# Gate sigmoids and attention tasks given a place in the issue order of an encoder block

## The chip, the cores and the metric

One Trainium2 chip, one of its cores. The metric is the device time of one execution in microseconds (us); times of a kernel are medians of several runs. The profile is of one execution, taken by the hardware profiler. A core has a matrix engine (TensorE, PE in the profile, with its weight loads as PEld), a vector engine (VectorE, DVE), a scalar engine for activation functions (ScalarE, ACT), a general one (GpSimd, POOL) and SyncE (SP), which issues transfers here. Each engine takes its instructions in the order of its own queue; between engines semaphores hold an instruction until its inputs are there.

## The reference

One layer of an encoder block on 256 tokens of width 2048, all in float32:

```
h = rmsnorm(x);  proj = h @ w_in          # q,k,v (sb) | q,k,v (ca) | gate_sb | gate_ca
y_sb = stick_breaking_attention(q, k, v)  # 8 heads of 128, strictly causal
y_ca = chunked_relpos_attention(q, k, v)  # 8 heads of 128, softmax with a relative bias
merged = sigmoid(gate_sb) * (y_sb @ w_sb_out) + sigmoid(gate_ca) * (y_ca @ w_ca_out)
x = x + merged @ w_mix_out
x = x + (silu(g) * u) @ w_ffn_out,  g, u = split(rmsnorm(x) @ w_ffn_in)
x = x + sigmoid(rmsnorm(x) @ w_ple_gate) * (p @ w_ple_in)
out = rmsnorm(x)
```

The stick-breaking weights are `exp(log_sigmoid(z) + sum of log_sigmoid(-z) over the keys between)`, so they need a logarithm and exponentials; the chunked attention needs the exponential of a softmax; the gates need sigmoids.

## The kernel before

**Pieces.** Every matmul with a weight matrix is cut into pieces of a weight: 256 x 512 or 512 x 256 numbers, 512 KB, loaded by SP into one of the `raw` buffers. To keep float32 precision a piece is split in two: ACT rounds it (`hi`, lines 270, 285, 288 and 291, the "weight casts"), DVE subtracts (`lo`, line 250 in `minus`), and PE does three products, high by high, low by high and high by low, in `three` (lines 299 to 301). `hi` and `lo` have three buffers each (line 245), a fourth in some stages.

**Kinds of groups.** `group("row", ...)` makes 512 output columns for all tokens with `three`. `group("feat", ...)` makes queries and keys with the features on the partitions; it issues its own two matmuls per tile (lines 373 and 375) and does not call `three`. `unit(...)` makes two blocks of 512 columns with one multiplication in eight saved for some pairs of pieces (Strassen's scheme, `split_pair` and `pair_products`); `su` are the accumulators of its own products, and it has more DVE work per matmul. A `gate_unit` is a unit that makes gate or value columns.

**Order in the code.** `flush(every)` goes through the pieces that are queued: `prefetch` loads and splits up to two pieces ahead, `products` issues the matmuls, and after every `every` pieces one entry of the list `tasks` is run, that is, its instructions are written there. With `in_turn=True` the entry's instructions are written inside `tc.issue_after(state["mm"].ins)`. That context adds an order edge: whatever the block writes for the same engine as the given instruction is queued behind it there. It is no wait for its result, and instructions of the block for other engines get no edge. `state["mm"]` is set in `three` (line 301) and, for the very first piece, in line 363. `state["cast"]` is set in `split` (line 270), to the last weight cast written.

**Order on the chip.** The framework plans each engine's queue before the program runs: it goes through the instructions with a model of their times, and an engine takes the earliest-written instruction that is ready in the model. An instruction that is ready long before its place in the code may so be queued far ahead of it. A load of an activation table (ACT_TABLE_LOAD in the profile) is put in front of an ACT instruction whose function is not in the set that is loaded at that point; the loads are shown under the line of that instruction. Line 83 loads the set `natural_log_exp_and_others` at the start.

**The stages around the change**, in the order of the code:
- the first gate group (lines 863 and 864), then queries and keys of the first stick-breaking half, `queries_and_keys(0, 0, sb_tasks)`, with `flush(4)`. When its last piece is done its attention is appended to `tasks` as six entries, `s1, s2, s3` for heads 0 and 1 and again for heads 2 and 3; the first of them is still run by this flush;
- a first `gate_unit` (values and gate columns), `flush(None)`: no tasks;
- `queries_and_keys(0, 1, ...)` and `(1, 0, ...)`, in whose flushes the other attention entries of the halves before are run (`flush(3)`, `flush(2.67)`, and `drain(6)` for what is left but the newest six);
- four more gate units, no tasks;
- `queries_and_keys(1, 1, ...)`, with the tasks of the first chunked half;
- the output projections `w_sb_out` (m = 0), with the tasks of the last chunked half, and `w_ca_out` (m = 1). After each group of 512 columns, `out_post(m, c)` writes two sigmoids (line 909), two products of the projection with the gate (line 911, DVE) and, for m = 1, the sum (line 914) and the transposes for the next stage.

The steps of the stick-breaking attention: `s1` makes the scores `zp` (PE), the absolute value, `Exp` and `Ln` (ACT, lines 708 to 710), then on DVE lines 712 and 713, and the split of the result; `s2` the sums over later keys (`bt`, lines 721 to 726), line 727 on DVE and an `Exp` (line 728); `s3` the weighted values `yp`. The chunked attention has one `Exp` step in `s1` (line 767, four instructions) and two transfers of the bias on POOL's queue.

Of the kernel before, what the change touches and what calls it, by code (L numbers as in the profile page):

```python
# [11 lines left out]
AF = mybir.ActivationFunctionType  # L12
# [33 lines left out]
def block_kernel(ctx: ExitStack, tc: tile.TileContext, x, p, w_in, w_sb_out, w_ca_out, w_mix_out,  # L46
# [18 lines left out]
    nc = tc.nc  # L65
# [81 lines left out]
    def run_task():  # L147
        name, fn = tasks.popleft()
        fn()
        if name is not None:  # L150
            done.add(name)

    def group(kind, wsrc, n0, kts, lhs, post, needs=lambda kt: None, row0=0, keep=None, after=None):

        ncol, nk = (NB, 2) if kind == "row" else (FB, 4)
        g = dict(kind=kind, post=post, lhs=lhs, ps=None, keep=keep, after=after)
        kts = list(kts)
        for j in range(0, len(kts), nk):
            part = kts[j : j + nk]
            r = (row0 + j) * P  # L160
            pieces.append(dict(
                g=g, kts=part, ncol=ncol, first=j == 0, last=j + nk >= len(kts),
                src=[wsrc[r : r + len(part) * P, n0 : n0 + ncol].rearrange("(k p) n -> p k n", p=P)],
                needs=[k for k in (needs(kt) for kt in part) if k is not None],
            ))
# [164 lines left out]
    def products(pc):  # L330
        g = pc["g"]
        if pc.get("pair"):
            pair_products(pc)
        elif g["kind"] == "unit":
            if pc["first"]:
                state["hold"] = g["hold"]
                g["ps"] = g.get("ps", []) + banks(g, g["pool"], "mm", 2)
            for i, kt in enumerate(pc["kts"]):
                a, z = pc["first"] and i == 0, pc["last"] and i == 1
                for t in range(2):  # L340
                    row_products(g["ps"][2 * pc["block"] + t], g["lhs"], kt, t, pc["hi"][:, i, :], pc["lo"][:, i, :], a, z)
            if g["after"] is not None and pc["block"] == 1:
                g["after"](pc["kts"])
            if pc["last"]:
                g["post"](g, pc["block"])
                state["hold"] = g["hold"] and pc["block"] == 0
        elif pc is pieces[1]:
            with tc.issue_after(state["mm"].ins):
                group_products(pc)
        else:  # L350
            group_products(pc)
        del pc["hi"], pc["lo"]
# [29 lines left out]
    state = dict(loaded=0, split=0, at=0, raw=0, hl=0, ext=0, ps=ps_mm, fourth=None, ring=0, places=0, hold=False)  # L382
# [6 lines left out]
    def prefetch():  # L389
        while state["loaded"] < len(pieces) and state["raw"] + len(pieces[state["loaded"]]["src"]) <= RAW + state["places"]:  # L390
            load(pieces[state["loaded"]])
            state["loaded"] += 1
        room = 2 if state["at"] < 4 + KD // 2 else 4 if state["fourth"] is not None else 3
        while state["split"] < state["loaded"] and state["split"] <= state["at"] + 3:
            pc = pieces[state["split"]]
            if state["split"] > state["at"] and sum(map(size, pieces[state["at"] : state["split"] + 1])) > room:
                break
            behind = [started["p"]]
            if pc["g"] is pieces[4]["g"]:
                behind += started.get(pc["kts"][0] - 2, [])  # L400
            with ExitStack() as order:
                for i in behind:
                    order.enter_context(tc.issue_after(i.ins))
                split(pc)
            state["split"] += 1

    def drain(left=0):
        while len(tasks) > left:
            run_task()

    def later(fn, n=3):

        for _ in range(n):
            tasks.append((None, lambda: None))
        tasks.append((None, fn))

    def flush(every=1, until=None, in_turn=False):

        n = 0
        while state["at"] < len(pieces) and (until is None or until not in done):  # L420
            pc = pieces[state["at"]]
            prefetch()
            products(pc)
            state["at"] += 1
            n += 1
            if tasks and every and not state["hold"] and int(n / every) > int((n - 1) / every):
                if in_turn:
                    with tc.issue_after(state["mm"].ins):
                        run_task()
                else:  # L430
                    run_task()
# [21 lines left out]
    def into_table(dst, c, src, gain=None, key=None, forms=None, pool=None, pairs=PAIRS):  # L453


        n = ps_ax[-1][1] // S if pool is None else 2
        for k0 in range(0, 4, n):
            ps = (aux("tp") if pool is None else late["ps"][pool].tile([P, 512], F32, tag="mm", name="tp"))
            ps = ps.rearrange("p (k s) -> p k s", k=n)
            for k in range(n):  # L460
                for t in range(NT):
                    nc.tensor.transpose(ps[:, k, t * P : (t + 1) * P], src[:, t, (k0 + k) * P : (k0 + k + 1) * P], ident)  # L462
            step = n if forms is None else 2
            for k1 in range(0, n, step):
                table_part(dst, 4 * c + k0 + k1, ps[:, k1 : k1 + step, :], gain, forms, pairs)
        for k in range(4):
            done.add((key, 4 * c + k))
# [335 lines left out]
    def queries_and_keys(mixer, b, make):  # L803
        c0 = mixer * 3 * W + b * NB
        qT, kT = (mp.tile([P, 4, S], F32, tag=f"{n}{b}", name=n) for n in ("qT", "kT"))
        for dst, off, sc in ((qT, 0, SCALE), (kT, W, None)):
            for j in range(2):
                then = None
                if off and j == 1:
                    then = lambda t=make(qT, kT, (mixer, b), 4 * b): push_attention(*t)  # L810
                group("feat", w2, c0 + off + j * FB, range(KD), T1, feat_post(dst, 2 * j, sc, then), needs=hneed)
# [67 lines left out]
    flush(None)  # L879
    state["fourth"] = None  # L880
    queries_and_keys(0, 1, sb_tasks)
    flush(3)
    drain(6)
    queries_and_keys(1, 0, ca_tasks)
    flush(2.67)
    drain(6)

    four_buffers(1)
# [7 lines left out]
    for c in range(4):  # L896
        dma_x.dma_start(x_[:, :, c * NB : (c + 1) * NB], xr[:, :, c * NB : (c + 1) * NB])
    queries_and_keys(1, 1, ca_tasks)
    flush(2.67)
    drain(6)  # L900
    work = mp.tile([P, 1024], F32, tag="v0", name="work")

    def out_post(m, c):
        def post(ps):
            cs = slice(c * NB, (c + 1) * NB)
            gt = gates[:, :, m, cs]
            for t in range(NT):
                by = rstd if (m, c) == (1, 0) else r1
                nc.scalar.activation(gt[:, t, :], gt[:, t, :], AF.Sigmoid, scale=by["mix"][:, t : t + 1])
            for t in range(NT):  # L910
                nc.vector.tensor_tensor(gates[:, t, m, cs], ps[t], gates[:, t, m, cs], ALU.mult)
            if m == 1:
                mg = gates[:, :, 0, cs]
                nc.vector.tensor_tensor(mg, mg, gt, ALU.add)
                later(lambda: into_table(T1, c, mg, key="mg", forms=lambda kt: FP[:, kt // 4 - 2], pairs=MIX_PAIRS))
        return post

    for m, wo in ((0, w_sb_out), (1, w_ca_out)):
        for c in range(4):
            group("row", wo[0], c * NB, range(8 * m, 8 * m + 8), T2, out_post(m, c), needs=lambda kt: ("y", kt))  # L920
        state["places"] = 0
        flush(2.67 if m == 0 else 1)


    def residual_done(c, key):
# [263 lines left out]
```

## Time and profile before

| | us |
|---|---|
| median of 3 runs | 1463.69 (1462.29 to 1463.74) |
| the profiled execution | 1464.04 |
| its span, first to last instruction | 1462.3 |
| PE busy | 1447.8 (99%) |
| DVE busy | 1242.2 (85%) |
| ACT busy | 819.6 (56%) |

The span is what the trace covers; some 1.7 us of the execution lie around it. Busy times of engines overlap. A row `line engine op out<-in` names the line of the code and the tiles that are written and read; `<-` behind a time in brackets names what ended the idle time. For PE the end of a matmul is modelled, and matmuls overlap, so the start times say more than the durations.

### The profile page before, as it was taken

To read this page: it belongs to the slowest core of one execution; us is meant where nothing else is said; L and a number is where in the kernel's file an instruction comes from. 1 tells how busy PE (TensorE), PEld (TensorE's weight loads), DVE (VectorE), ACT (ScalarE), POOL (GpSimd) and SP (SyncE) were. 2 spreads that over 40 slices of the span, in tenths; PEclk is the share of its full clock that TensorE was granted. 3 is DMA by queue.
4 is the path that set the end of the run, shared out by engine and by line. 5 is a ranking of instruction groups with operands and counts; after the bars stand their busy time and mean duration, and the time that the engine had idled before them with its cause. 6 is when DMAs were issued, how large, how long until landed. Compare 5 with 4: busy or idle time off the path is not lost.

```text
span 1462.3 us, 18695 instructions
## 1 busy us (share of the span) xinstructions
PE 1447.8 (99%) x6849; PEld 1210.3 (83%) x6849; DVE 1242.2 (85%) x1570; ACT 819.6 (56%) x966; POOL 22.5 (2%) x44
## 2 busy tenths in 40 slices
PE   9999999999999999999999999999999999999997
PEld 7887888788888888888888888888888888888886
DVE  6978777998877777888999999999999989999775
ACT  6546567656555544565555555555645555565552
POOL 0100000000000000000000000000000000000000
PEclk9999999999999999999999999999999999999999
DMA  9865555566675555765666666666666666666672
GB/s 319 274 204 177 185 168 171 171 211 204 199 254 164 179 166 181 229 198 177 195 194 188 195 208 214 196 195 209 195 199 202 203 190 198 216 197 210 229 228 72
DMA packets 164731, 291.17 MB, mean 199 GB/s; under 512 B 9024, under 2 KB 42096, under 8 KB 164384
## 3 DMA queue, kind: packets, MB, share of 16 engines
q1 hardware_dynamic: 162528, 281.32, 61.5%
q0 software_dynamic: 2112, 8.68, 1.8%
q8 instruction: 53, 0.87, 0.3%
q14 instruction: 38, 0.31, 0.1%
HBM read 284.19 MB, written 5.77 MB: 198 GB/s over the span
## 4 chain that ended last, share of the span: by engine, by line
PE 96%; DMA 2%; ACT 1%; DVE 1%; issue 0%; SPq 0%; DVEq 0%; ACTq 0%
PE mm L300 23%; PE mm L301 23%; PE mm L299 23%; PE mm L373 8%; PE su L300 4%; PE su L301 4%; PE su L299 4%; PE mm L375 4%; PE tp L462 1%; DMA raw<-in_w_in 1%; DMA raw<-in_w_ple_in 1%; ACT hi L270 0%; DMA raw<-in_w_mix_out 0%; DVE lo L250 0%; PE yp L689 0%
## 5 line engine op out<-in xcount | busy, mean ns | idle before, releaser
L250 DVE TENSOR_TENSOR lo<-raw,hi 128x1024 fp32r<-128x1024 f32 (+1 forms) x517 | 625.7, 1218 | 131.1 <-ACT hi L270 120.8
L270 ACT CAST hi<-raw 128x1024 fp32r<-128x1024 f32 (+1 forms) x387 | 405.1, 1050 | 399.3 <-PE mm L301 299.0
L300 PE MATMUL mm<-lo,T 128*128 128x512 f32 x1349 | 526.2, 390 | 1.2 <-DVE lo L250 1.2
L301 PE MATMUL mm<-hi,T 128*128 128x512 f32 x1349 | 522.2, 390 | 0.0
L299 PE MATMUL mm<-hi,T 128*128 128x512 f32 x1349 | 500.4, 391 | 1.4 <-ACT hi L270 1.3
L299 PEld LDWEIGHTS mm<-hi,T 128*128 128x128 f32 x1349 | 252.9, 188 | 54.1 <-ACT hi L270 2.3
L300 PEld LDWEIGHTS mm<-lo,T 128*128 128x128 f32 x1349 | 253.3, 188 | 53.4 <-DVE lo L250 1.6
L301 PEld LDWEIGHTS mm<-hi,T 128*128 128x128 f32 x1349 | 253.3, 188 | 52.4
L373 PE MATMUL mm<-T,hi 128*128 128x512 f32 x512 | 180.4, 398 | 0.0
L375 PE MATMUL mm<-T,lo 128*128 128x256 f32 x512 | 140.3, 280 | 0.0
L373 PEld LDWEIGHTS mm<-T,hi 128*128 128x128 f32 x512 | 95.1, 188 | 20.7
L288 ACT CAST hi<-raw 128x1024 fp32r<-128x1024 f32 x65 | 68.5, 1053 | 77.2 <-DVE raw L250 25.4
L250 DVE TENSOR_TENSOR T<-xf,T 128x1536 fp32r<-128x1536 f32 x58 | 101.7, 1754 | 10.4 <-ACT T L291 10.4
L250 DVE TENSOR_TENSOR xf<-raw 128x512 f32<-128x512 f32 x130 | 89.1, 685 | 14.9 <-DMA raw<-in_w_ffn_in 4.2
L375 PEld LDWEIGHTS mm<-T,lo 128*128 128x128 f32 x512 | 96.6, 189 | 1.7
L291 ACT CAST T<-xf 128x1536 fp32r<-128x1536 f32 x58 | 85.9, 1480 | 18.8 <-DVE xf L250 18.1
L285 ACT CAST hi<-raw 128x1024 fp32r<-128x1024 f32 x65 | 68.5, 1053 | 31.5 <-PE mm L301 24.9
L834 DVE TENSOR_TENSOR C<-su,C 128x512 f32<-128x512 f32 x72 | 47.6, 682 | 0.3
L838 DVE TENSOR_TENSOR C<-mm,C 128x512 f32<-128x512 f32 x72 | 46.6, 680 | 0.0
L250 DVE TENSOR_TENSOR xf<-raw,xf 128x512 f32<-128x512 f32 x65 | 44.5, 685 | 0.4
L250 DVE TENSOR_TENSOR raw<-raw 128x512 f32<-128x512 f32 x65 | 44.5, 684 | 0.2
L301 PE MATMUL mm<-T,T 128*128 128x512 f32 (+1 forms) x90 | 33.4, 371 | 0.0
(326 smaller groups left out, 1448.0 us busy)
## 6 DMA issues: line engine op xcount, KB each, us to landing
raw<-in_w_ffn_in SPq DMA_DIRECT2D x176, 512.0 KB, 4.0
raw<-in_w_in SPq DMA_DIRECT2D x160, 512.0 KB, 4.3
raw<-in_w_ffn_out SPq DMA_DIRECT2D x88, 512.0 KB, 4.6
raw<-in_w_mix_out SPq DMA_DIRECT2D x32, 512.0 KB, 4.6
raw<-in_w_ple_gate SPq DMA_DIRECT2D x32, 512.0 KB, 4.9
raw<-in_w_sb_out SPq DMA_DIRECT2D x16, 512.0 KB, 4.0
raw<-in_w_ca_out SPq DMA_DIRECT2D x16, 512.0 KB, 3.9
x<-in_x SPq DMA_DIRECT2D x4, 512.0 KB, 10.4
```

Source lines behind the costliest of these rows:

```text
L250: return nc.vector.tensor_tensor(out, a, b, ALU.subtract)
L270: state["cast"] = nc.scalar.copy(hi[:, c : c + m], raw[:, c : c + m])
L285: nc.scalar.copy(h1, raw1)
L288: nc.scalar.copy(h2, raw2)
L291: nc.scalar.copy(xh, xf)
L299: nc.tensor.matmul(ps, xh, hi, start=a, stop=False)
L300: nc.tensor.matmul(ps, xh, lo, start=False, stop=False)
L301: state["mm"] = nc.tensor.matmul(ps, xl, hi, start=False, stop=z)
L373: nc.tensor.matmul(ps, hi[:, i, f], lhs[:, kt, :, :].rearrange("p c s -> p (c s)"), start=a, stop=False)
L375: nc.tensor.matmul(ps[:, :S], lo[:, i, f], lhs[:, kt, 0, :], start=False, stop=z)
L834: nc.vector.tensor_tensor(C[i], q, C[j], ALU.add)
L838: nc.vector.tensor_tensor(g["C"][i], g["ps"][i], g["C"][i], ALU.add)
```

## The change

Three calls of `flush` in the attention stages get `in_turn=True`, and that of the output projections for m = 0. The sigmoids of `out_post` are written behind the last weight cast.

```diff
     queries_and_keys(0, 1, sb_tasks)
-    flush(3)
+    flush(3, in_turn=True)
     drain(6)
     queries_and_keys(1, 0, ca_tasks)
-    flush(2.67)
+    flush(2.67, in_turn=True)
     drain(6)
...
     queries_and_keys(1, 1, ca_tasks)
-    flush(2.67)
+    flush(2.67, in_turn=True)
     drain(6)
...
             for t in range(NT):
                 by = rstd if (m, c) == (1, 0) else r1
-                nc.scalar.activation(gt[:, t, :], gt[:, t, :], AF.Sigmoid, scale=by["mix"][:, t : t + 1])
+                with tc.issue_after(state["cast"].ins):
+                    nc.scalar.activation(gt[:, t, :], gt[:, t, :], AF.Sigmoid, scale=by["mix"][:, t : t + 1])
...
         state["places"] = 0
-        flush(2.67 if m == 0 else 1)
+        flush(2.67 if m == 0 else 1, in_turn=m == 0)
```

## The prediction

> **What bounds the kernel now.** I read the page first, then the list of what TensorE (PE) waited for, in the whole run and between 100 and 300 us, and then the timeline around each wait.
>
> ```profile
> span 1462.3 us, 18695 instructions
> PE 1447.8 (99%) x6849; PEld 1210.3 (83%) x6849; DVE 1242.2 (85%) x1570; ACT 819.6 (56%) x966; POOL 22.5 (2%) x44
> ```
> ```profile
> PE warm L560 <- POOL mhalf L101: 1.2, 1, 1.2
> ```
> ```profile
> PE mm L299 <- ACT hi L270: 1.3, 1, 1.3
> PE mm L300 <- DVE lo L250: 1.2, 1, 1.2
> PE su L299 <- ACT hi L285: 0.8, 1, 0.8
> PE su L300 <- DVE lo L250: 0.8, 1, 0.8
> ```
>
> PE is busy for 99% of the span. The change leaves every matmul in the program, so it can win only what PE idles in the part of the run that it touches. The second fence is the one row of the whole run that names another wait (the warm-up at the start); the third has the stretch that holds the attention tasks of the first mixer. There are four waits in it: 1.29 + 1.21 + 0.80 + 0.79 = 4.09 us. That is the ceiling of the gain: 0.28% of 1464.04 us, the time of the profiled execution. An effect of 0.2%, 2.9 us, is about what a measurement of this kernel can tell from no change, so even a complete success is hardly above it.
>
> Three of the four waits lie at the start of the first gate unit. These are the timelines there of ScalarE (ACT), VectorE (DVE) and PE; columns are start, duration, instruction and, in brackets, idle time before it and what ended it.
>
> ```profile
> 115.85 0.37 ACT L437 COPY tm<-mm 128x256 f32<-128x256 f32 x1 [1.26 <-DVE sm L439]
> 116.24 1.28 ACT L709 ACT_TABLE_LOAD   x1
> 117.53 0.85 ACT L709 ACTIVATE e<-e 128x768 f32<-128x768 f32 x1
> 118.40 1.28 ACT L710 ACT_TABLE_LOAD   x1
> 119.69 0.85 ACT L710 ACTIVATE e<-e 128x768 f32<-128x768 f32 x1
> 120.44 1.03 ACT L285 CAST hi<-raw 128x1024 fp32r<-128x1024 f32 x1
> ```
> ```profile
> 113.05 0.69 DVE L250 TENSOR_TENSOR xf<-raw 128x512 f32<-128x512 f32 x1 [3.62 <-DMA raw<-in_w_in]
> ...
> 116.67 1.22 DVE L250 TENSOR_TENSOR lo<-raw,hi 128x1024 fp32r<-128x1024 f32 x1
> ...
> 118.40 0.42 DVE L439 TENSOR_TENSOR sm<-mm,tm 128x256 f32<-128x256 f32 x1
> 120.57 0.96 DVE L712 SCALAR_TENSOR_TENSOR ls<-zp,e 128x768 f32<-128x768 f32 x1 [1.75 <-ACT e L710]
> 121.44 0.41 DVE L645 TENSOR_TENSOR kT<-sm,rbc 128x256 f32<-128x256 f32 x1
> 121.78 1.22 DVE L250 TENSOR_TENSOR lo<-raw,hi 128x1024 fp32r<-128x1024 f32 x1
> ```
> ```profile
> 120.11 0.39 PE L300 MATMUL mm<-lo,T 128*128 128x512 f32 x1
> 120.34 0.39 PE L301 MATMUL mm<-hi,T 128*128 128x512 f32 x1
> 121.52 0.50 PE L299 MATMUL su<-hi,T 128*128 128x512 f32 x1 [0.80 <-ACT hi L285]
> 121.86 0.39 PE L299 MATMUL mm<-hi,T 128*128 128x512 f32 x1
> 123.05 0.50 PE L300 MATMUL su<-lo,T 128*128 128x512 f32 x1 [0.79 <-DVE lo L250]
> ```
>
> The reader is to see a queue. The first attention step's exponential and logarithm each carry a table load, the cast that PE needs (L285) stands behind both, and on DVE the low half that PE needs next (121.78) stands behind an instruction (L712) that waits 1.75 us for that logarithm. The fourth wait has the same form at the start of the second gate unit:
>
> ```profile
> 271.00 1.28 ACT L728 ACT_TABLE_LOAD   x1
> 272.30 0.85 ACT L728 ACTIVATE ls<-ls 128x768 f32<-128x768 f32 x1
> 273.05 1.03 ACT L270 CAST hi<-raw 128x1024 fp32r<-128x1024 f32 x1
> ```
> ```profile
> 274.13 0.74 PE L299 MATMUL mm<-hi,T 128*128 128x512 f32 x2 [1.29 <-ACT hi L270]
> ```
>
> **The change: the sigmoids.** The 16 sigmoids have their inputs long before they are needed, and run as soon as these are there (14 in a row below, the other two behind the load at 69.4 us). The instructions of the lines concerned, with counts, durations, first and last start:
>
> ```profile
> L83 ACT ACT_TABLE_LOAD  x1: 1283/1283/1283, 0.8 to 0.8; - x1
> ```
> ```profile
> L909 ACT ACTIVATE gates<-gates,r_mix x14: 708/717/727, 160.3 to 429.7; 128x512 f32<-128x512 f32 x14
> L909 ACT ACT_TABLE_LOAD  x3: 1283/1283/1283, 69.4 to 343.7; - x3
> ```
> ```profile
> L710 ACT ACT_TABLE_LOAD  x4: 1283/1283/1283, 118.4 to 253.8; - x4
> ```
> ```profile
> L728 ACT ACT_TABLE_LOAD  x4: 1283/1283/1283, 168.8 to 271.0; - x4
> ```
> ```profile
> L767 ACT ACT_TABLE_LOAD  x1: 1283/1283/1283, 441.8 to 441.8; - x1
> ```
>
> Line 83 loads a set named for logarithm and exponential together. Nothing replaces it until the first sigmoid, at 69.4 us; from there on each logarithm of L710 and each exponential of L728 loads anew, so what is then loaded for the one does not hold the other. With the edge to the weight casts no sigmoid can be issued before the output projections, which come after all steps that use a logarithm. I take it that the set of line 83 then serves them: 3 loads of L909, 1 of L709, 4 of L710, 4 of L728 and 1 of L767 go, 13 x 1.283 = 16.7 us of ACT. Most of it lies beside PE's matmuls and is worth nothing. What counts is what stands in front of a wait:
>
> 1. First gate unit, second and third wait. Without the two loads the logarithm ends at 116.24 + 0.85 + 0.85 = 117.94 instead of 120.54, and L285 may run from there to 118.97. The second wait (0.80) goes: PE starts `su` one issue distance (120.34 - 120.11 = 0.23) after its last matmul, at 120.57. DVE takes L712 when `sm` is done, 118.8, then `kT` to 120.1 and the low half to about 121.3; PE's next `lo` matmul starts at 121.3 + 0.05 instead of 123.05. That is 1.7 us earlier. What is late next is this low half, still 0.3 us behind PE.
> 2. First wait, 1.21 us. It ends with the low half at 116.67, before any load could delay DVE; DVE had been held up to 113.05 by a transfer of weights. Bounds: 0 and 1.21 us gained. I take 0, since that row is nearest and the change does not touch it.
> 3. Second gate unit. Without the load the cast starts 1.28 us earlier, at 271.77, and PE's wait of 1.29 us goes. The attention steps ahead of it also come earlier, by one load or two each. Gain 1.3 us, bounds 0 (another instruction takes the place) and 1.3.
>
> Their sum is 3.0 us, with bounds 0 and 4.1.
>
> What is added: 16 x 0.717 = 11.5 us of sigmoids in the projections, most of it between 478 and 545 us. The window and its costliest groups on ACT:
>
> ```profile
> 478.00:545.00 67.00, 67.00 (x326) 56.28 (x326) 48.32 (x69) 32.27 (x51) 1.26 (x3) 1.00 0.57 175
> ```
> ```profile
> L270 ACT CAST hi<-raw 128x1024 fp32r<-128x1024 f32 x22 | 23.1, 1051 | 24.2 <-PE mm L301 23.4 <-ACT hi L270 0.8
> L767 ACT ACTIVATE zs<-zs,mx 128x256 f32<-128x256 f32 (+1 forms) x8 | 3.5, 445 | 0.9 <-DVE mx L764 0.9
> ```
>
> PE (first pair of numbers) has no idle time there and ACT (fourth) is busy for 32.27 of 67 us. Ten sigmoids (four groups of the first projection, one of the second) bring 7.2 us. The softmax steps of the last four heads fall between them, twice, so there are at most five loads (sigmoid, exponential, sigmoid, exponential, sigmoid), 6.4 us: together 45.9 of 67 us. An edge gives order only; the sigmoid waits for no new result. Behind it on ACT stand the next casts, and on DVE the product of L911, which needs it, with the next low half behind. The cover is the distance at which casts run ahead: 22 casts in 67 us are 3.05 us for a piece, and with three buffers a cast has two pieces, 6.1 us, less 1.05 for itself and about 1.2 for its low half (DVE at 116.67): 3.8 us. A sigmoid pair with its load, 2.7 us, fits. I take 0 for it; without the cover it costs up to what the rival below says.
>
> [...]
>
> **The attention tasks.** The edge goes to `state["mm"]`, which only `three` sets (and the first piece), and the "feat" groups of queries and keys do not call `three`. (The step at 116 us belongs to the flush before the first gate unit, which is not changed.) In three of the four flushes the edge thus points to the last matmul of the gate unit before. Does it hold anything back? The first task matmul in such a flush, and the unit's last before it:
>
> ```profile
> L721 PE MATMUL bt<-sh,below x2: 387/391/395, 167.3 to 198.6; 128*128 128x512 f32 x2
> ```
> ```profile
> 159.15 0.39 PE L301 MATMUL mm<-hi,T 128*128 128x512 f32 x1
> ```
>
> The task comes 8 us after it, so the edge is already kept. The tasks' other engines get no edge, and their transfers (two for each softmax step, on POOL's queue) are not moved. In the fourth flush, the first projection, the edge is at its place; there the tasks are late by their own inputs. I take 0, bounds +-0.5 us (about one matmul).
>
> **Sum.** 1464.04 - 3.0 = 1461.0 us for the profiled execution; the median of the runs shown, 1463.69, is 0.35 lower, so 1460.7 us for a median.
>
> **Rivals.**
> - **Only the second unit gains.** DVE is the bound at the first one: beside its two waits (3.62 and 1.75 us) it has the low halves, the sums of the attention step and the end of the keys to do in order, and another order of its instructions may put the low half behind something else. Then 1463.7 - 1.3 = 1462.4.
> - **The first wait closes too**, since DVE and ACT are emptied earlier and the planner places the low half sooner: 1463.7 - 4.1 = 1459.6. For it: it is the same place and queue. Against: the transfer at 113.05.
> - **The loads stay**, because an exponential asks for its own set whatever is loaded. For it: in this trace none ever ran on the set of line 83. Against: from 0.8 to 69.4 us copies, squares and scalings ran on it with no other load, so a set stays while it serves. No change, 1463.7.
> - **The projections pay** (the other side). Where a softmax step meets a sigmoid pair, ACT has 1.28 + 1.43 + 1.28 + 1.8 (four of L767) = 5.8 us between two casts, less the 1.1 us that it idled per cast (24.2 / 22): 4.7 us late, and the products of L911 (about 1.4 us) stand before the low half as well. Against 3.8 us of cover that is 2.3 us of PE for a meeting, 4.6 for two: 1460.7 + 4.6 = 1465.3, slower than before. It decides from the point where the cast is more than 3.8 us late. With item 1 lost as well it is 1467.0. Against it: ACT's 24.2 us of idle time in the window.
>
> **How the numbers follow.** Forecast (1460.7) 0.40; only the second unit 0.22; first wait too 0.15; loads stay 0.12; projections pay 0.11. The bound for faster, 1463.7 - 2.9 = 1460.8, lies at the forecast itself: a little over half of its 0.40 is beyond it, with the 0.15 and a rest of the second case 0.42 faster. Slower by over 0.2% needs 1466.6: most of the last rival with item 1 lost, and what a new order by the planner can do, 0.09. Within 0.2%: 0.49. Range: 1459.0 (the ceiling, and 0.6 for the spread of the runs) to 1465.3.
>
> **What would show it.** Right: no table load between 0.8 us and the projections, none at L710 and L728, waits for L285 and at about 272 us gone, a wait of about 1.2 us for a low half left near 117 us, three to five loads in the projections and no PE wait there. Wrong: loads still at L710; the waits replaced by others at the unit starts; PE waits for L270 or L250 between 478 and 600 us; attention matmuls in another order against the pieces.

## The result, and the profile after

| | before | after |
|---|---|---|
| median, us (19 runs each, on the same chip) | 1463.61 (1462.29 to 1465.73) | 1460.10 (1459.42 to 1462.13) |
| ratio of the times | | 0.9977, 95% interval 0.9970 to 0.9984 |
| the profiled execution, us | 1464.04 | 1460.55 |
| its span, us | 1462.3 | 1458.8 |

The changed kernel is faster by 3.5 us, 0.23% by the ratio. The forecast was 1460.7 us. The ratios, here and below, come from all runs, and as a few runs of the experiments and of the kernel before beside them took some 10 us more at a lower mean clock (0.994 to 0.996), a ratio need not be the quotient of the two medians. Behind line 909 its lines are numbered one higher: the sigmoid is now L910 and its product L912.

These are two lines of the page after, and under them the one row that the list of PE's waits between 100 and 300 us still holds.

```profile
span 1458.8 us, 18690 instructions
PE 1446.6 (99%) x6849; PEld 1210.4 (83%) x6849; DVE 1241.2 (85%) x1570; ACT 809.5 (55%) x958; POOL 22.4 (2%) x44
```
```profile
PE mm L300 <- DVE lo L250: 1.6, 1, 1.6
```

PE has as many matmuls as before, and ACT has eight instructions fewer: 966 against 958. Of four waits one is left, the first of the first gate unit. It even grew, from 1.21 to 1.63 us.

The eight instructions are table loads. In the list of instruction groups of ACT in the whole run after, these are all rows with loads (count, busy us and mean ns behind the name):

```profile
L910 ACT ACT_TABLE_LOAD x3 | 3.8, 1283 | 0.1
L767 ACT ACT_TABLE_LOAD x2 | 2.6, 1283 | 0.0
L83 ACT ACT_TABLE_LOAD x1 | 1.3, 1283 | 0.8 <-PEq L1179 0.8
L1015 ACT ACT_TABLE_LOAD x1 | 1.3, 1283 | 1.0 <-PE mm L301 1.0
L1089 ACT ACT_TABLE_LOAD x1 | 1.3, 1283 | 1.2 <-PE mm L301 1.2
L1113 ACT ACT_TABLE_LOAD x1 | 1.3, 1283 | 0.0
```

Before there were 17, now there are 9. L709, L710 and L728, the exponentials and logarithms of the stick-breaking attention, have none. The sigmoids and the softmax steps (L910, L767) have five, all in the output projections. The row of L83 and the last three are in the kernel before as well, the last three under line numbers lower by one.

The timelines of ACT, DVE and PE at the start of the first gate unit, after (start, duration, instruction, idle time before it and what ended it):

```profile
116.11 0.38 ACT L437 COPY tm<-mm 128x256 f32<-128x256 f32 x1 [1.68 <-DVE sm L439]
116.38 0.85 ACT L709 ACTIVATE e<-e 128x768 f32<-128x768 f32 x1
117.26 0.84 ACT L710 ACTIVATE e<-e 128x768 f32<-128x768 f32 x1
118.01 1.04 ACT L285 CAST hi<-raw 128x1024 fp32r<-128x1024 f32 x1
```
```profile
113.32 0.69 DVE L250 TENSOR_TENSOR xf<-raw 128x512 f32<-128x512 f32 x1 [3.37 <-DMA raw<-in_w_in]
...
116.93 1.22 DVE L250 TENSOR_TENSOR lo<-raw,hi 128x1024 fp32r<-128x1024 f32 x1
...
119.00 0.95 DVE L712 SCALAR_TENSOR_TENSOR ls<-zp,e 128x768 f32<-128x768 f32 x1
...
120.19 1.22 DVE L250 TENSOR_TENSOR lo<-raw,hi 128x1024 fp32r<-128x1024 f32 x1
```
```profile
118.20 0.50 PE L300 MATMUL mm<-lo,T 128*128 128x512 f32 x1 [1.63 <-DVE lo L250]
...
120.62 0.39 PE L301 MATMUL mm<-hi,T 128*128 128x512 f32 x1
120.85 0.39 PE L299 MATMUL su<-hi,T 128*128 128x512 f32 x1
121.07 0.39 PE L299 MATMUL mm<-hi,T 128*128 128x512 f32 x1
121.47 0.50 PE L300 MATMUL su<-lo,T 128*128 128x512 f32 x1
```

The exponential stands directly behind the copy, and the logarithm behind the exponential. The cast of L285 starts at 118.01 instead of 120.44. Its first matmul on PE starts at 120.85, 0.23 us after the one before it. DVE takes L712 without idle time, and the next low half starts at 120.19 instead of 121.78. The matmul at 121.47 comes 0.40 us after the one before it, where 0.23 is the usual distance.

The second gate unit after, ACT and PE:

```profile
269.32 0.84 ACT L728 ACTIVATE ls<-ls 128x768 f32<-128x768 f32 x1
270.06 1.04 ACT L270 CAST hi<-raw 128x1024 fp32r<-128x1024 f32 x1
```
```profile
270.65 1.23 PE L299 MATMUL mm<-hi,T 128*128 128x512 f32 x4
```

The exponential has no load ahead of it, and PE has no idle time.

The output projections as a table by window: us, then busy time and count of PE, weight loads, DVE, ACT and POOL, the granted clock, the DMA share and GB/s. The first row is the window of the prediction.

```profile
478.00:545.00 67.00, 67.00 (x326) 56.28 (x325) 47.41 (x65) 44.02 (x64) 1.27 (x3) 1.00 0.57 169
470.00:620.00 150.00, 150.00 (x716) 125.35 (x715) 114.69 (x148) 90.38 (x122) 1.27 (x3) 1.00 0.62 191
```

ACT is busy for 44.0 of 67 us, against 32.3 before. PE has no idle time in either window.

**Where the 3.5 us of the span came from.** PE has 6849 matmuls in both profiles, so the start of the n-th in the one can be set against the start of the n-th in the other. By 113 us the changed kernel leads by 0.2 us, at 130 us by 1.6, at 258 us still by 1.6, at 280 us by 3.0, at 590 us still by 3.0, at 612 us by 3.6 and at the end by 3.5. The first gate unit thus gave 1.4 us, the second 1.4, a stretch near 600 us 0.55, and the start of the run 0.2. The last is the start-up of one execution against another.

### The profile page after: what moved, and what is told of

Read it like the earlier page. It is cut to its first block, busy times and chain, and to the rows that moved or that the text cites. A ratio compares the mean times of both kernels' runs of the same rounds, so it can differ in the third digit from the quotient of the medians.

```text
span 1458.8 us, 18690 instructions
## 1 busy us (share of the span) xinstructions
PE 1446.6 (99%) x6849; PEld 1210.4 (83%) x6849; DVE 1241.2 (85%) x1570; ACT 809.5 (55%) x958; POOL 22.4 (2%) x44
## 4 chain that ended last, share of the span: by engine, by line
PE 97%; DMA 1%; DVE 1%; ACT 0%; issue 0%; SPq 0%; DVEq 0%
PE mm L300 23%; PE mm L301 23%; PE mm L299 23%; PE mm L373 8%; PE su L300 4%; PE su L299 4%; PE su L301 4%; PE mm L375 4%; PE tp L462 1%; DMA raw<-in_w_in 1%; DMA raw<-in_w_ple_in 1%; DVE lo L250 0%; PE yp L689 0%; PE xps L516 0%; ACT hi L270 0%
## 5 line engine op out<-in xcount | busy, mean ns | idle before, releaser
L250 DVE TENSOR_TENSOR lo<-raw,hi 128x1024 fp32r<-128x1024 f32 (+1 forms) x517 | 627.0, 1222 | 133.3 <-ACT hi L270 123.1
L270 ACT CAST hi<-raw 128x1024 fp32r<-128x1024 f32 (+1 forms) x387 | 405.5, 1052 | 407.5 <-PE mm L301 289.4
L250 DVE TENSOR_TENSOR T<-xf,T 128x1536 fp32r<-128x1536 f32 x58 | 102.0, 1758 | 10.4 <-ACT T L291 10.4
L250 DVE TENSOR_TENSOR xf<-raw 128x512 f32<-128x512 f32 x130 | 89.6, 690 | 13.4 <-DMA raw<-in_w_ffn_out 3.6
L285 ACT CAST hi<-raw 128x1024 fp32r<-128x1024 f32 x65 | 68.6, 1055 | 33.8 <-PE mm L301 28.1
L834 DVE TENSOR_TENSOR C<-su,C 128x512 f32<-128x512 f32 x72 | 47.8, 686 | 0.3
L250 DVE TENSOR_TENSOR xf<-raw,xf 128x512 f32<-128x512 f32 x65 | 44.8, 689 | 0.4
L250 DVE TENSOR_TENSOR raw<-raw 128x512 f32<-128x512 f32 x65 | 44.8, 690 | 0.2
```

The source lines that it names most:

```text
L250: return nc.vector.tensor_tensor(out, a, b, ALU.subtract)
L270: state["cast"] = nc.scalar.copy(hi[:, c : c + m], raw[:, c : c + m])
L285: nc.scalar.copy(h1, raw1)
L834: nc.vector.tensor_tensor(C[i], q, C[j], ALU.add)
```

## The experiments

All ratios are against the kernel before, on the same chip and in the same comparison. The diffs are against the changed kernel, if nothing else is said.

### 1. Without the sigmoids' edge: what the attention tasks give

```diff
-                with tc.issue_after(state["cast"].ins):
-                    nc.scalar.activation(gt[:, t, :], gt[:, t, :], AF.Sigmoid, scale=by["mix"][:, t : t + 1])
+                nc.scalar.activation(gt[:, t, :], gt[:, t, :], AF.Sigmoid, scale=by["mix"][:, t : t + 1])
```

> The changed kernel without the edge on the sigmoids, so the four edges on the attention tasks alone. Theory (the gain is the table loads that stood in front of casts): these edges hold nothing back, every engine's queue is that of the kernel before, ratio 1.000, 1463.6 us, the four PE waits of 1.2, 0.8, 0.8 and 1.3 us unchanged. Rival (the tasks' place matters): a good part of the 3.5 us, 1460 to 1462 us.

Measured: 1463.75 us, ratio 0.9993 (0.9975 to 1.0011). All four waits are there:

```profile
PE mm L299 <- ACT hi L270: 1.3, 1, 1.3
PE mm L300 <- DVE lo L250: 0.8, 1, 0.8
PE su L299 <- ACT hi L285: 0.8, 1, 0.8
PE su L300 <- DVE lo L250: 0.8, 1, 0.8
```

The edges of the attention tasks change nothing, and the reason can be read without a clock: in this kernel every engine has the same queue of instructions as in the kernel before. The kernel with the sigmoids' edge alone has the same queues as the changed one, so it needed no run. The whole gain belongs to the sigmoids.

### 2. The loads put back, the sigmoids left late

A load of the sigmoids' set is put behind the last weight cast before the first gate unit, so that the attention no longer finds the set of line 83. The sigmoids stay in the projections.

```diff
+    with tc.issue_after(state["cast"].ins):
+        nc.scalar.preload_act_table_set("sigmoid_and_others")
```

> The changed kernel with one more table load behind the first gate group: the set of the sigmoid is loaded there, so that all exponentials and logarithms of the first mixer load again, while the sigmoids stay in the projections. Theory (loads): nine loads return at L709, L710 and L728, with the PE waits for L285 and its low half (0.8 and 0.8 us) and at the second gate unit (1.3 us); 1463.0 us, 2.9 slower than the changed kernel, ratio to the kernel before 0.9996. Rival (what counts is that the sigmoids' own 11.5 us of ScalarE left the gate units): 1460.1 us, ratio 0.9977.

Measured: 1464.21 us, ratio 1.0004 (0.9988 to 1.0021), 1.2 us more than was expected (its profile has a stretch of 3.40 us at a clock of 0.50 behind the waits, shown in the last section). Between 100 and 300 us PE waits again:

```profile
PE mm L299 <- ACT hi L270: 1.3, 1, 1.3
PE su L300 <- DVE lo L250: 0.8, 1, 0.8
PE su L299 <- ACT hi L285: 0.8, 1, 0.8
PE mm L300 <- DVE lo L250: 0.5, 1, 0.5
```

L709 has one load again, L710 and L728 four each. That the early sigmoids are gone from that part brings no gain that these runs show; the loads that they caused are the cost.

### 3. The sigmoids left early, the set put back

Here the kernel before gets two loads more: the set for exponential and logarithm together, after the first and after the last sigmoids that stand ahead of the attention steps. This diff is against the kernel before.

```diff
-                nc.scalar.activation(gt[:, t, :], gt[:, t, :], AF.Sigmoid, scale=by["mix"][:, t : t + 1])
+                sig = nc.scalar.activation(gt[:, t, :], gt[:, t, :], AF.Sigmoid, scale=by["mix"][:, t : t + 1])
+            if (m, c) in ((1, 0), (0, 0)):
+                with tc.issue_after(sig.ins):
+                    nc.scalar.preload_act_table_set("natural_log_exp_and_others")
```

> The kernel before, sigmoids where they were, with the set for logarithm and exponential loaded again behind the first two pairs of sigmoids (about 71 and 161 us). Two loads are added, the nine of L709, L710 and L728 go. Theory (loads): the same gain as the change or nearly, 1460.3 us, ratio 0.9978, no wait for L285 and none at the second gate unit. Rival (the sigmoids' place): 1463.6 us, ratio 1.000.

Measured: 1460.54 us, ratio 0.9973 (0.9953 to 0.9993). One wait is left between 100 and 300 us, as after the change:

```profile
PE mm L300 <- DVE lo L250: 1.0, 1, 1.0
```

Two added loads (the x2 of its line 912 below; the x3 of line 909 are the sigmoids' own, as before) take away the nine of L709, L710 and L728.

```profile
L909 ACT ACT_TABLE_LOAD x3 | 3.8, 1283 | 0.1
L912 ACT ACT_TABLE_LOAD x2 | 2.6, 1283 | 0.0
```

The gain is the changed kernel's within the intervals, with every sigmoid where it was. So, as far as these intervals tell, it does not matter whether the sigmoids run early or late, only which set they leave behind. While the set for exponential and logarithm was in place, neither asked for a load: there is none at L709, L710 or L728 here and after the change, with four instructions at each of these lines. Once a sigmoid had replaced it, the kernel before loaded for every logarithm (four loads at L710) and for every exponential of L728 (four), 1.283 us each.

### 4. More loads in the projections: how deep the cover is

Loads of the exponential's and the sigmoids' set are put ahead of each group's two sigmoids, once (2 loads) and three times (6 loads).

```diff
+            with tc.issue_after(state["cast"].ins):
+                for _ in range(3):     # and range(1)
+                    nc.scalar.preload_act_table_set("exp_and_others")
+                    nc.scalar.preload_act_table_set("sigmoid_and_others")
```

> The changed kernel with two more table loads (2.6 us of ScalarE) ahead of each pair of sigmoids in the output projections, where the run with six waited. Theory (a cover of about 3.8 us beside 1.1 us of idle time in front of a cast): 2.6 + 1.4 us, and 1.3 us more where an exponential had its set loaded, fit in 4.9 us except where the softmax step of 3.1 us with its load meets them, twice: 0 to 4 us slower than the changed kernel, 1460 to 1464 us. Rival (no cover: each added load is paid): 8 times 2.6 us, 1481 us.

> The changed kernel with six more table loads (7.7 us of ScalarE) ahead of each pair of sigmoids in the output projections, eight times. It measures the cover there. By the prediction's reckoning a cast has 3.8 us of cover and 1.1 us of idle time before it: 7.7 + 1.4 - 1.1 = 8.0 us late against 3.8 us of cover, 4.2 us of PE waits for each of 8 pairs, 34 us, 1494 us. If the cover is larger than reckoned (casts catch up over several pieces, ScalarE being busy for half of the window): much less, 1460 to 1475 us.

Measured, with two loads: 1463.10 us, ratio 0.9992 (0.9976 to 1.0009), 3.0 us above the changed kernel. PE's waits between 470 and 620 us:

```profile
PE mm L299 <- ACT hi L270: 1.0, 1, 1.0
PE mm L300 <- DVE lo L250: 0.7, 1, 0.7
```

Both lie at 524 to 526 us, where a softmax step (L767) meets a sigmoid pair. The other meeting, near 490 us, and the pairs alone are covered. Three pairs of the changed kernel had a load of their own, whose place one of the added ones takes, so there are 13 more loads in the projections (18 against 5), and PE waits 1.7 us in all. Set against the same matmuls of the changed kernel, this one loses 2.2 us at 523 to 530 us and 0.4 us near 600 us, which is most of the 3.0. The profiled execution lay only 1.5 us above the changed kernel's by its span, since its first wait of the first gate unit was 0.9 us shorter.

Measured, with six loads: 1503.65 us, ratio 1.0264 (1.0236 to 1.0292), 43.5 us above the changed kernel. The two largest rows of its waits in the whole run, and the windows of the projections and of a stretch in them (columns as above):

```profile
PE mm L299 <- ACT hi L270: 22.2, 7, 5.7
PE mm L300 <- DVE lo L250: 2.7, 4, 1.4
```
```profile
470.00:620.00 150.00, 123.93 (x530) 98.63 (x530) 78.02 (x103) 123.19 (x140) 1.26 (x3) 0.90 0.41 126
497.70:500.00 2.30, 2.30 (x8) 1.75 (x7) 1.32 (x6) 2.30 (x8) 0.00 (x0) 0.51 0.75 227
```

Here the cover is gone, and PE waits for the casts of L270, as the rival "the projections pay" had it. PE is idle for 26 of the 150 us of the first window, less than the 34 us that were expected. For a pair that is about 3.3 us (26 / 8), and not the 43.5 / 8 = 5.4 that the time says. Most of the rest is the clock, which the expectation did not have: it is 0.90 over the 150 us and 0.51 in the second row, where PE has no idle time at all. These are matmuls of that execution:

```profile
495.48 0.73 PE L299 MATMUL mm<-hi,T 128*128 128x512 f32 x2 [2.10 <-ACT hi L270]
496.74 0.50 PE L300 MATMUL mm<-lo,T 128*128 128x512 f32 x1 [0.52 <-DVE lo L250]
...
497.80 0.63 PE L299 MATMUL mm<-hi,T 128*128 128x512 f32 x1
498.23 0.63 PE L300 MATMUL mm<-lo,T 128*128 128x512 f32 x1
```

After waits of 2.10 and 0.52 us the matmuls follow each other at 0.43 us instead of 0.23, for some 3.4 us; it happened seven times, twice for 6.8 us. In the seven stretches of 20 us from 480 to 620 us the clock was 0.94, 0.97, 0.88, 0.86, 0.91, 0.91 and 0.74, in sum about 31 us at half clock (an estimate from these seven means). Once the cover was used up here, a late cast cost its wait and then the clock.

### 5. The wait that is left

The prediction had named a transfer as the cause of the first wait, and gave the change no part in it. Over all profiles with that order of instructions, DVE's first instruction behind the transfer and the end of PE's wait are:

| kernel | DVE resumes, us | PE resumes, us | PE had waited, us |
|---|---|---|---|
| experiment 2 | 112.09 | 116.98 | 0.47 |
| experiment 1 | 112.29 | 117.18 | 0.84 |
| experiment 4, two loads | 112.34 | 117.23 | 0.69 |
| experiment 4, six loads | 112.87 | 117.76 | 1.42 |
| experiment 3 | 112.88 | 117.76 | 1.01 |
| before | 113.05 | 117.94 | 1.21 |
| after | 113.32 | 118.20 | 1.63 |

PE resumes 4.88 or 4.89 us after DVE in each of the seven, with loads at L709 or without. With this order of instructions the end of the wait is set by when this piece of the weights lands, and that differs by 1.2 us between executions. Four kernels changed the order at this place. First, the first attention step written behind the gate unit instead of ahead of it:

```diff
     queries_and_keys(0, 0, sb_tasks)
-    flush(4)
+    flush(4.01)
```

> The changed kernel with the first attention step of heads 0 and 1 written after the first gate unit instead of before it. It asks what the wait is that is left at 116.6 us (1.2 to 1.6 us). Theory A (the step's scores hold one of the two accumulators that the unit needs, and its pieces and low halves come in another order for it): the wait goes, 1458.6 us, unless the later steps now run into the second gate unit. Theory B (a transfer of weights that lands late holds VectorE, whatever the order): the wait stays between 0.8 and 1.7 us, 1460.1 us.

Measured: 1462.33 us, ratio 0.9995 (0.9981 to 1.0008). The first gate unit has no wait at all, but between 100 and 300 us stand instead:

```profile
PE mm L300 <- DVE lo L250: 1.1, 1, 1.1
PE yp L677 <- ACT sh L671: 0.5, 1, 0.5
```

The first is at the start of the second gate unit (276.35), the second two microseconds on, and just behind 300 us PE waits twice more, 0.9 us in sum, for DVE at L834. Every step of this attention now comes later, and the last ones run into the next unit, as theory A had allowed. DVE resumed at 112.09 us here, as in experiment 2, where PE waited 0.47 us: the transfer alone does not make the wait, the work that DVE has behind it does its part. Second, the same step one group earlier:

```diff
-    def queries_and_keys(mixer, b, make):
+    def queries_and_keys(mixer, b, make, at=1):
...
-                if off and j == 1:
+                if off and j == at:
...
-    queries_and_keys(0, 0, sb_tasks)
-    flush(4)
+    queries_and_keys(0, 0, sb_tasks, at=0)
+    flush(3.4)
```

> The changed kernel with the first attention step written two pieces earlier in the flush before the first gate unit. Its scores move forward by less than that (they wait for the keys): their last matmuls stand half a piece earlier in PE's queue, so the accumulator is free some 1 us earlier. Theory A: the wait at 116.6 us shrinks by up to 1 us, 1459.1 to 1460.1 us. Theory B: no difference, 1460.1 us.

Measured: 1461.96 us, ratio 0.9994 (0.9982 to 1.0006). Neither theory foretold the result. The wait is not smaller but larger:

```profile
PE mm L300 <- DVE lo L250: 2.5, 1, 2.5
PE su L299 <- ACT hi L288: 0.7, 1, 0.7
```
```profile
119.44:122.85 3.41, 3.41 (x10) 2.63 (x9) 3.41 (x4) 0.70 (x1) 0.00 (x0) 0.50 0.48 156
```

The transfer lands no earlier (DVE resumes at 113.53), and PE resumes 5.41 us after it instead of 4.89, since one more of the differences (L250, 0.69 us) now stands ahead of the low half, in place of a shorter instruction of the keys. The second fence shows a clock of 0.50 for 3.41 us after the wait. Third and fourth, another order of the pieces in the first gate unit, by a parameter `order` that only its call uses: the pair of pieces whose differences DVE has to form stands later, or one block of plain pieces first.

```diff
-             slots, mid, post, hneed, alone=pool, order=GATE_ORDER)
+             slots, mid, post, hneed, alone=pool, order=order)
...
+               add_values((0, 1)), order=(0, 0, 1, 1, 3, 3, -2, -4, 5, 5, -6, 7, 7))
```
```diff
+               add_values((0, 1)), order=(0, 1, 0, 1, *GATE_ORDER[4:]))
```

> The changed kernel with another order of pieces in the first gate unit alone: the first combined pair after six single pieces instead of four. The differences that VectorE makes for this pair, and the transfer they wait for until 113.3 us, so no longer stand ahead of the low half that PE waits for. Theory B (that transfer, in VectorE's queue): the wait of 1.2 to 1.6 us at 116.6 us goes, 1458.6 us. Theory A (the accumulator held by the attention step): the second block still cannot start until about 122 us, the single pieces use up the buffers, and the wait stays or grows, 1460 to 1462 us.

> The changed kernel with another order of the first four pieces of the first gate unit: two of its first block, then two of its second, where it was one of each in turn. PE already takes the two of the first block first, since an accumulator of the second is held by the attention step's scores until about 122 us; the low half of the second block's first piece, which no matmul can use by then, stands at 113.9 us ahead of the one that PE waits for at 116.6 us. Theory A (the held accumulator puts the low halves in the wrong order): the wait at 116.6 us goes, a shorter one of 0 to 0.8 us comes at about 119 to 121 us, 1458.6 to 1459.6 us. Theory B (the late transfer alone): the low half is still behind the transfer's 113.3 us, but at 113.9 to 115.1 it is soon enough; so B also gives a gain here and differs from A in the run with the step behind the unit, which had no wait with the transfer landing at 112.1. If neither holds, the wait stays at 1.2 to 1.6 us, 1460.1 us.

Measured: 1460.62 us, ratio 0.9978 (0.9968 to 0.9989), with waits of 0.98 us (to 117.94) and 0.86 us (to 121.81); and 1460.01 us, ratio 0.9978 (0.9969 to 0.9987), with one wait of 1.20 us (to 121.19). In the fourth kernel the wait near 117 us is gone, as both theories had it, but the later one is longer than the 0.8 us that theory A allowed. No gain over the changed kernel (0.9977) shows in either. DVE in the fourth kernel shows why:

```profile
113.04 0.69 DVE L250 TENSOR_TENSOR xf<-raw 128x512 f32<-128x512 f32 x1 [3.36 <-DMA raw<-in_w_in]
113.65 1.22 DVE L250 TENSOR_TENSOR lo<-raw,hi 128x1024 fp32r<-128x1024 f32 x1
114.78 0.68 DVE L250 TENSOR_TENSOR raw<-raw 128x512 f32<-128x512 f32 x1
...
119.58 0.42 DVE L645 TENSOR_TENSOR kT<-sm,rbc 128x256 f32<-128x256 f32 x1
119.92 1.22 DVE L250 TENSOR_TENSOR lo<-raw,hi 128x1024 fp32r<-128x1024 f32 x1
```

From 113.04 to 121.14 DVE has no idle time (only the first line has a bracket, and none of the lines left out has one). What it could not do in the 3.36 us ahead of the transfer it has to make up, and an order of the pieces only chooses which low half is late. None of these kernels beats the changed one. A transfer issued earlier, or one more buffer for the pieces, was not tried.

## Why the prediction was right, step by step

- **The set of line 83 serves once no sigmoid comes between: right.** It was taken from the order of the loads in the trace of before. Experiments 2 and 3 show it from both sides (nine loads at L709, L710 and L728 in the one, none in the other), and the rival "the loads stay" is out. Eight loads went in sum: the 13 named, and five new ones in the projections, as many as the working allowed at most.
- **Item 1, the first gate unit: right.** Both waits (0.80 and 0.79) are gone. The low half was to be 0.3 us behind PE still; it is 0.17 us behind (0.40 less the usual 0.23). The gain was put at 1.7 us and came to 1.4 in the profiled executions, since the first wait was 0.42 us longer in the later one. It was longer because DVE resumed 0.27 us later after the transfer (113.32 against 113.05).
- **Item 2, the first wait stays: right**, and for the reason given, by the fixed 4.89 us of the table above. The rival "the first wait closes too" is out, and that DVE binds at this place, the ground of the rival "only the second unit gains", is right for this wait alone.
- **Item 3, the second gate unit: right.** The wait of 1.29 us is gone; the stretch gained 1.4 us. A little more than the idle time goes with a wait, because the list counts from the modelled end of the last matmul: from 120.34 to 121.52 us in the kernel before are 1.18 us, 0.95 over the usual 0.23, and the row gives 0.80. The ceiling of 4.09 us, a sum of idle times, was therefore too low by roughly 0.15 us for each of its four waits.
- **The sigmoids in the projections cost nothing: right.** ACT was reckoned at 45.9 of 67 us and is at 44.0; PE has no wait there. The cover, however, had less to hold than the rival "the projections pay" feared: its 5.8 us between two casts never came about. At the first meeting a cast runs between the sigmoids and the softmax step (at 488.45 us), and at the second the sigmoids need no load, so that ACT is away from the casts for 4.4 us (517.05 to 521.45). In experiment 4 with two loads the second meeting takes 7.0 us (516.12 to 523.12) and PE waits 1.0 us for a cast, so a stretch of some 6 us is covered there (an estimate, 7.0 less 1.0), against 4.9 reckoned (3.8 and 1.1 of idle time). What the rival left out is the clock: its 2.3 us for a meeting counts the wait alone, and with six loads a clock of 0.90 over 150 us is some 15 of the 43 us.
- **The attention edges cost nothing: right**, exactly so by the queues.
- **What the sum did not have:** the stretch near 600 us, where the last pieces of the output projections pass into the next stage. There the kernel before had a gap in PE and some longer distances between matmuls; 0.55 us of these are gone. Set against the kernel before in the same way, experiments 2 and 3 gain 0.6 and 0.7 us there, and experiment 1, which has the queues of the kernel before, 0.1. The gain thus comes with late sigmoids and with early ones, with the attention's loads and without. The order of the casts there differs from the kernel before in the changed kernel; which part of the order does it was not tested.

The sum was 3.0 us and the span lost 3.5: the two gate units gave 2.85, that stretch 0.55 and the start 0.2, and 0.05 were lost on the way. So part of the closeness is luck. The transfer of item 2 happened to land later in the profile after than in any of the other six of the table, which cost 0.4 us against the profile before, and the stretch that the sum did not have made up for it.

One reservation concerns the medians. Of the 20 runs of the kernel before beside the last experiment, six had a mean granted clock of 0.997 and took 1464.2 to 1465.2 us; the other 14 (0.998 or 0.999) took 1462.6 to 1463.7. The changed kernel was never under 0.998 in 19 runs. The 1.6 us between the medians of the two groups is what one stretch of 3.41 us at half clock would cost (an estimate, 3.41 / 2 = 1.7). In the two other sets, of 29 runs of the kernel before, the medians of such groups lie 1.6 us apart as well, though the groups overlap there. Experiment 2, with two waits of 0.79 us where the kernel before has 0.80 and 0.79, shows such a stretch in its profile, at 122.89 right behind them, and loses 1.6 us there against the same matmuls of the kernel before. Its profile and that of the step one group earlier are the only two at 0.997, and the eight at 0.998 or 0.999 have no such stretch behind a wait. So part of the gain in the median (3.5, against about 3.0 when only the runs of the kernel before at 0.998 or more are taken) may be that the waits no longer slow the clock now and then. For the kernel before this was not seen in a trace, since its profiled execution had no such stretch there; it stays an inference.

## What to carry to other kernels

A function on ScalarE cost more here than its own time of 0.72 us: in the kernel before the sigmoids replaced a set with which the steps after them run without a load (none in experiment 3), and nine loads of 1.283 us followed at L709, L710 and L728. Look for the first load of a foreign set, and either move that function behind the last user or load the shared set again by hand; experiment 3 did that with two added instructions for the same gain. A table load was worth what stood behind it in its engine's queue with another engine waiting for it: of the thirteen loads that went, three set three of PE's waits (0.80, 0.79 and 1.29 us).

## What the runs showed of the hardware that was not expected

PE's granted clock fell to half after quite short waits: after 0.79 + 0.79 us within 3.4 us (experiment 2), after 2.5 us (the step one group earlier), and after 2.10 + 0.52 us (six loads). It was 0.50 for 3.41 us in the step one group earlier and for 3.40 us in experiment 2, and with six loads the stretches were some 3.4 us long, two of them 6.8. Distances between matmuls rose from 0.23 to 0.43 us. These are the windows of experiment 2 ahead of the fall and behind it:

```profile
119.48:122.89 3.41, 1.82 (x7) 0.97 (x6) 3.28 (x5) 3.36 (x4) 0.00 (x0) 1.00 0.12 47
122.90:126.30 3.40, 3.40 (x9) 2.63 (x8) 3.40 (x6) 1.88 (x2) 0.00 (x0) 0.50 0.54 159
```

PE was busy for 1.82 of the 3.41 us ahead of the fall. A single wait of 1.63 us (after the change) left the clock at 1.00 in its profile, and so did 0.80 + 0.79 us in the profile of before. What decides whether the clock falls was not measured.
